# Plain float32 output projections and query products in a two-layer diffusion block, with the low parts of the blocks done ahead on VectorE

## The chip, the cores and the metric

The kernel runs on one core of one Trainium2 chip. The metric is the device time of one execution in microseconds; the numbers shown are medians of several executions, and one execution was also taken by the hardware profiler. The core has five engines with a queue of instructions each: TensorE (PE; its weight loads appear as PEld), VectorE (DVE), ScalarE (ACT), GpSimd (POOL) and SyncE (SP). An engine takes its queue in order; engines wait for one another through semaphores, and data is moved by 16 DMA engines.

## The reference

A backbone with two layers over 512 latent tokens and 256 context tokens of 1024 numbers, all in float32. Layer 0 mixes tokens by a state-space model (S5), layer 1 by latent attention with 8 heads (MLA). Behind each mixer stands an output projection, a residual layer norm, and a channel mixer (PEER) that picks 16 of 16384 experts for each of 8 heads. Cut to what matters here:

```python
def s5_output(y, w_glu, w_o):
    y = gelu(y)
    return (y * sigmoid(y @ w_glu)) @ w_o            # output projection of layer 0
o_lat = attend(...).reshape(b, n, 1024) @ w_o         # output projection of layer 1
h = layer_norm(ALPHA * h + mod[2] * o, ln_g, ln_b)

def peer_route(t, w_q, keys):                         # t = h * (1 + mod[4]) + mod[3]
    q = (t @ w_q).reshape(n, 8, 2, 64)                # queries
    s = einsum('thsd,hsnd->thsn', q, keys)
    sv, si = top_k(s, 16)                             # per half, then over the 256 sums
    ...                                               # expert indices e, gates g = softmax
act = gelu(einsum('td,tkd->tk', t, u[e])) * g
out = einsum('tk,tkd->td', act, v[e])
```

Tokens are worked on in six tiles of 128: tiles 0 and 1 are the context (in layer 0 alone), 2 to 5 the latent tokens.

## The kernel before

**Split products.** A product on TensorE can be made from float32 operands as they are (plain), or from operands in a reduced float32 form (`F32R`). For accuracy the kernel splits an operand for the second way into a high part, a cast on ScalarE (L305), and a low part, the operand less the high part (L306), on an engine that the caller names. `split` holds both lines:

```python
        self.nc.scalar.copy(out=hi, in_=x)
        lo_eng.tensor_tensor(out=lo, in0=x, in1=hi.bitcast(F32), op=ALU.subtract)
```

A split product is then three products into one accumulator: high by high, high by low and low by high.

**Experts.** Some token tiles get their experts by gathering rows with indirect DMAs that GpSimd issues (L1275), a row for each token and expert; VectorE multiplies each row (L1282 for `u`, L1287 for `v`). The others are dense: their scores against all 16384 experts are computed in 128 blocks (`dense_u`, L1137, split products), multiplied with a gate matrix that is made from one-hots (`gate_matrix`: VectorE makes `e` at L1080 and `o` at L1088, TensorE multiplies them at L1102), and multiplied with all of `v` (L1207). Layer 0 gathers tiles 0 and 1 and has tiles 2 to 5 dense; layer 1 gathers tile 5 and has 4, 2 and 3 dense.

**Ahead.** The scores of the first 40 (layer 0) or 48 (layer 1) dense blocks are done ahead, while routing and the gate matrices still run (`ahead`, two blocks of preload). For each, U is loaded, its high part cast by ScalarE and its low part made by GpSimd. The later blocks, in the dense stage, have theirs made by VectorE (`dense_u_prep` with `V`).

**Output projection** (`out_steps`), for a pair of tiles: a first step splits the operands of the pair (`ys` in layer 0 with low parts on GpSimd, `os` in layer 1 with low parts on VectorE). Then 16 steps, two column halves by eight blocks of k: load 128x512 of the weights (`wo`, ring of 8 buffers), split it (`Wos`, low part on VectorE for every fourth step, else GpSimd), three products for each tile of the pair (L799). VectorE multiplies each finished half with a row (L806), and a last step does the residual and the layer norm on VectorE and ScalarE.

**Queries** (`query_steps`), for a pair: `modulate` transposes and modulates each tile's `h` (`mT`) and splits it into the block `Hs` that the dense stage uses too (for the context, into a block `Hc` of its own). Then for each of 8 heads: load 128 columns of weights (`wq`, ring `row` of 5 buffers, which the gathered rows use too), split them with GpSimd's low part, and 24 products of 256 columns, both tiles of the pair side by side (L945).

**Order.** `pipeline(steps, LT)` runs the loads and splits of a step three steps before its products. The list of steps is written out by hand: in layer 0 the projections `o0` (context), `o1` (tiles 2, 3) and `o2` (tiles 4, 5), the gates `g2` to `g5` of the mixer, modulations `m` and heads `q`, with constants E0, E1, E2, YB and YC saying where one list is cut to let another in. `merge` interleaves this stream with the routing of the tiles (`route`, almost all on VectorE: the top-16 searches L972 to L976 and one-hots L1041 to L1047), and, on the side, the blocks ahead and the gate matrices, by estimated times that steps return. The compiler's scheduler then orders each engine's queue; routing, norms, splits and one-hots share VectorE's.

Of the kernel before, what the change touches and what calls it, by code (L numbers as in the profile page):

```python
# [21 lines left out]
KD = 8  # L22
# [33 lines left out]
E0, E1, E2 = 0, 11, 5  # L56
YB, YC = 1, 17
# [50 lines left out]
class Net:  # L108
# [662 lines left out]
    def out_steps(self, l, pair, src, parts, first, rows):  # L771

# [3 lines left out]

        def begin(_):
            st["y"] = parts()
            return 0.0

        def prep(hf, k):
            if (hf, k) == (1, 0):
                st["h"] = []
                for ti in pair:
                    h = self.t4([128, D], "h")
                    self.load(h, first(ti))
                    st["h"].append(h)
            w = self.t2([128, 512], "wo")
            self.load(w, src[k * 128:(k + 1) * 128, hf * 512:(hf + 1) * 512])
            W = self.t4([128, 2, 512], "Wos", F32R)  # L790
            self.split(W[:, 0], W[:, 1], w, nc.gpsimd if k % 4 else nc.vector)
            return W

        def work(hf, k, W):
            if k == 0:
                st["op"] = [self.ps([128, 512], "op") for _ in pair]
            for i, op in enumerate(st["op"]):
                for n, (x, y) in enumerate(((0, 0), (0, 1), (1, 0))):
                    nc.tensor.matmul(out=op, lhsT=st["y"][k // 2][:, x, k % 2, i * 128:(i + 1) * 128], rhs=W[:, y],  # L799
                                     start=(k == 0 and n == 0), stop=(k == KD - 1 and n == 2))  # L800
            if k == KD - 1:
                if hf == 0:
                    st["t"] = [self.t4([128, D], "res") for _ in pair]
                c = slice(hf * 512, (hf + 1) * 512)
                for t, op in zip(st["t"], st["op"]):
                    nc.vector.tensor_tensor(out=t[:, c], in0=op, in1=rows()[0][:, c], op=ALU.mult)  # L806
            return 1.3

        def norm(_):
            for ti, h, t in zip(pair, st["h"], st.pop("t")):  # L810
# [7 lines left out]
        return ([(lambda: None, begin)]  # L818
                + [(lambda hf=hf, k=k: prep(hf, k), lambda W, hf=hf, k=k: work(hf, k, W)) for hf in range(2) for k in range(KD)]
                + [(lambda: None, norm)])  # L820

    def s5_layer(self, dense, gather):
# [25 lines left out]
        def out(pair):  # L848
            s = 1 if pair[0] < 2 else 0
            per = (2, 4)[s]  # L850
            r0 = pair[0] * 128 - (256, 0)[s]

            def parts():
                ys = []
                for x in range(4):
                    ys.append(self.t4([128, 2, 2, 256], "ys", F32R))
                    y = self.yT[s][2 * x // per][:, 2 * x % per:2 * x % per + 2, r0:r0 + 256]
                    self.split(ys[-1][:, 0], ys[-1][:, 1], y, nc.gpsimd)
                return ys

            return self.out_steps(0, pair, a["s5_w_o"], parts,
# [16 lines left out]
        Hc = self.t16([128, 2, KD, 256], "Hc", F32R)  # L878
        self.h1 = {}
        (m0, q0), (m1, q1), (m2, q2) = (self.query_steps(0, (0, 1), lambda: Hc),  # L880
# [5 lines left out]
        steps += g4 + g5[:2 - YB] + o1[:1] + g5[2 - YB:]  # L886
        steps += [(lambda: None, memory)] + o1[1:YC] + o2[:1] + o1[max(YC, 1):] + o2[1:E1] + m1 + o2[E1:] + q1[:E2] + m2 + q1[E2:] + q2
# [20 lines left out]
    def query_steps(self, l, pair, H):  # L908
# [7 lines left out]
        def modulate(i, ti):  # L916
            mT = self.mod_transpose(self.h1[pair][i], l, s, 3)
            c = slice(i * 128, (i + 1) * 128)
            H_ = H()
            self.split(H_[:, 0, :, c], H_[:, 1, :, c], mT, nc.vector)  # L920
            if ti not in self.tiles:
# [8 lines left out]
        def prep(h):  # L930
            w = self.row([128, KD, 128], "wq")
            self.load(w, self.a["peer_w_q"][l, h])
            W = [self.t4([128, KD, 128], f"wq{x}", F32R) for x in range(2)]
            self.split(W[0], W[1], w, nc.gpsimd)
            return W

        def work(h, W):
# [4 lines left out]
            n = 0  # L942
            for k in range(KD):
                for x, y in ((0, 0), (0, 1), (1, 0)):
                    PE.matmul(out=st["p"][:, h % 2], lhsT=W[x][:, k, :], rhs=H()[:, y, k, :], start=(n == 0),  # L945
                              stop=(n == 3 * KD - 1))
                    n += 1
# [195 lines left out]
    def ahead(self, l, n, n_tiles):  # L1143
# [12 lines left out]
        yield from pipeline([(lambda b=b: self.dense_u_prep(l, b, self.nc.gpsimd), lambda Us, b=b: work(b, Us))  # L1156
# [180 lines left out]
    def mla(self, dense, gather):  # L1337
# [181 lines left out]
        def out(pair):  # L1519
            q0 = (min(pair) - 2) * 128  # L1520

            def parts():
                os = []
                for o in oT:
                    os.append(self.t4([128, 2, 2, 256], "os", F32R))
                    for i, ti in enumerate(pair):
                        c = slice(i * 128, i * 128 + 128)
                        self.split(os[-1][:, 0, :, c], os[-1][:, 1, :, c], o[:, :, (ti - 2) * 128:(ti - 1) * 128], V)
                return os

            return self.out_steps(1, pair, a["mla_w_o"], parts, lambda ti: self.hd[ti], lambda: r)
# [91 lines left out]
```

## Time and profile before

| what | value |
|---|---|
| median of 3 executions | 4076.9 us (4074.23 to 4081.48) |
| the profiled execution's own time | 4075.69 us |
| its span | 4073.6 us |
| busy share of the span: PE, PEld, DVE, ACT, POOL | 90%, 74%, 79%, 38%, 40% |
| mean granted TensorE clock (share of full speed) | 0.953 |
| DMA | 986.15 MB, 242 GB/s over the span |

The span falls into stages: the state-space mixer of layer 0 until about 374 us; gates, projections and queries of layer 0 with the first routings until 657; routing of the dense tiles with blocks ahead until 855; gate matrices and blocks ahead until 1110; the dense stage until about 2350; the attention of layer 1 until 2672; its projections and queries until 2765; routing until 2975; gate matrices until 3165; the dense stage until the end.

How to read the views. The table of stretches gives the busy time of each engine in a stretch, the granted TensorE clock and the mean busy share of the 16 DMA engines. A group of instructions has a line, engine, operation, names and shape, a count, its busy time and the mean of one, and the idle time of the engine just before its members with what ended most of it. The timeline has start, length, engine, line, operation, names and shape, with like neighbours merged (x is their count) and the idle time before them in brackets. A plain float32 product shows as two records of TensorE.

### The profile page before, as it was taken

To read this page: it belongs to the slowest core of one execution; us is meant where nothing else is said; L and a number is where in the kernel's file an instruction comes from. 1 tells how busy PE (TensorE), PEld (TensorE's weight loads), DVE (VectorE), ACT (ScalarE), POOL (GpSimd) and SP (SyncE) were. 2 spreads that over 40 slices of the span, in tenths; PEclk is the share of its full clock that TensorE was granted. 3 is DMA by queue.
4 is the path that set the end of the run, shared out by engine and by line. 5 is a ranking of instruction groups with operands and counts; after the bars stand their busy time and mean duration, and the time that the engine had idled before them with its cause. 6 is when DMAs were issued, how large, how long until landed. Compare 5 with 4: busy or idle time off the path is not lost.

```text
span 4073.6 us, 54069 instructions
## 1 busy us (share of the span) xinstructions
PE 3664.2 (90%) x18795; PEld 3029.0 (74%) x18795; DVE 3231.9 (79%) x6315; ACT 1558.1 (38%) x2804; POOL 1638.1 (40%) x1140
## 2 busy tenths in 40 slices
PE   5759879789789999999999989989888899999998
PEld 3527868678667888778888855568888678999997
DVE  8784498988877788988888844469987678888887
ACT  1321335357632322233332233354467333433333
POOL 4744346245412455556555300055344113334341
PEclk6879989899999999999999999999899999999999
DMA  5457234268988899999999820044377888887885
GB/s 178 136 175 249 86 122 156 90 220 272 326 302 293 300 341 342 332 352 340 338 336 342 324 103 3 30 160 149 126 232 256 316 277 321 295 336 283 335 294 215
DMA packets 398450, 986.15 MB, mean 242 GB/s; under 512 B 67040, under 2 KB 147424, under 8 KB 393568
## 3 DMA queue, kind: packets, MB, share of 16 engines
q1 hardware_dynamic: 217120, 501.34, 35.3%
q0 software_dynamic: 110592, 402.70, 28.0%
q10 hardware_dynamic: 70464, 78.65, 5.6%
q8 instruction: 148, 2.42, 0.2%
q14 instruction: 126, 1.03, 0.1%
HBM read 892.28 MB, written 90.21 MB: 241 GB/s over the span
## 4 chain that ended last, share of the span: by engine, by line
PE 45%; issue 10%; DVE 10%; DMA 5%; POOL 5%; ACT 3%; ACTq 0%; POOLq 0%; DVEq 0%; SPq 0%
PE s_ps L1137 20%; PE acc L1207 15%; POOL row L1275 4%; PE g_ps L1102 3%; DMA row<-in_peer_v,idx 2%; DMA W<-in_peer_v 1%; DVE row L1282 1%; PE op_mla L1507 1%; DMA ge<-ged 1%; DVE e L1080 1%; DVE Ws L306 1%; PE acc L1228 1%; DVE f L1287 1%; PE kvp L1365 1%; ACT o L1085 1%
## 5 line engine op out<-in xcount | busy, mean ns | idle before, releaser
L1207 PE MATMUL acc<-Ws,A 128*128 128x512 f32 x5208 | 1202.9, 392 | 63.6 <-ACT A L305 36.3
L1137 PE MATMUL s_ps<-Hs,Uh 128*128 128x512 f32 (+1 forms) x4096 | 1184.8, 371 | 11.2 <-ACT Uh L305 11.2
L1207 PEld LDWEIGHTS acc<-Ws,A 128*128 128x128 f32 x5208 | 981.8, 189 | 280.4 <-ACT A L305 37.0
L1137 PEld LDWEIGHTS s_ps<-Hs,Uh 128*128 128x128 f32 x4096 | 761.5, 190 | 104.9 <-ACT Uh L305 12.6
L1275 POOL DMA_INDIRECT row<-in_peer_u,idx x384 | 513.2, 1336 | 783.2 <-DVE row L1282 712.3
L1137 PE MATMUL s_ps<-Hs,Ul 128*128 128x512 f32 (+1 forms) x2048 | 756.9, 370 | 15.5 <-POOL Ul L306 15.5
L1275 POOL DMA_INDIRECT row<-in_peer_v,idx x384 | 485.6, 1264 | 549.0 <-DVE f L1287 484.8
L1282 DVE SCALAR_TENSOR_TENSOR row<-row,m 128x1024 f32<-128x1024 f32 x384 | 490.4, 1293 | 54.7 <-DMA row<-in_peer_u,idx 53.8
L1287 DVE SCALAR_TENSOR_TENSOR f<-row,act,f 128x1024 f32<-128x1024 f32 x381 | 487.3, 1279 | 39.4 <-DMA row<-in_peer_v,idx 38.4
L305 ACT CAST Ws<-W 128x512 fp32r<-128x512 f32 x512 | 305.5, 619 | 489.0 <-DMA W<-in_peer_v 439.5
L1137 PEld LDWEIGHTS s_ps<-Hs,Ul 128*128 128x128 f32 x2048 | 389.0, 190 | 66.2 <-POOL Ul L306 19.8
L306 DVE TENSOR_TENSOR Ws<-W,Ws 128x512 fp32r<-128x512 f32 x512 | 345.1, 684 | 101.6 <-ACT Ws L305 101.0
L305 ACT CAST Uh<-U 128x1024 fp32r<-128x1024 f32 x256 | 268.1, 1048 | 313.6 <-DMA U<-in_peer_uT 242.6
L306 POOL TENSOR_TENSOR Ul<-U,Uh 128x1024 fp32r<-128x1024 f32 x88 | 227.3, 2585 | 312.3 <-ACT Uh L305 199.0
L1140 ACT ACTIVATE ge<-s_ps 128x512 f32<-128x512 f32 (+1 forms) x256 | 139.1, 544 | 520.4 <-PE s_ps L1137 504.9
L1102 PE MATMUL g_ps<-o,o 128*128 128x128 f32 x1792 | 232.7, 289 | 87.2 <-DVE o L1088 51.7
L1102 PEld LDWEIGHTS g_ps<-o,o 128*128 128x128 f32 x1792 | 223.7, 202 | 96.9 <-ACT o L1085 95.1
L306 POOL TENSOR_TENSOR Wos<-wo,Wos 128x512 fp32r<-128x512 f32 x60 | 87.0, 1476 | 469.9 <-PE tp_ps L286 350.9
L305 ACT CAST A<-ge 128x512 fp32r<-128x512 f32 (+1 forms) x256 | 144.5, 565 | 280.7 <-DVE ge L1188 266.6
L306 DVE TENSOR_TENSOR Ul<-U,Uh 128x1024 fp32r<-128x1024 f32 x168 | 204.9, 1221 | 47.9 <-ACT Uh L305 47.5
L1188 DVE TENSOR_TENSOR ge<-ge,Gt 128x512 f32<-128x512 f32 (+1 forms) x256 | 155.7, 619 | 74.8 <-ACT ge L1140 51.1
L306 DVE TENSOR_TENSOR A<-ge,A 128x512 fp32r<-128x512 f32 (+1 forms) x256 | 158.4, 620 | 45.6 <-ACT A L305 44.7
(346 smaller groups left out, 4631.7 us busy)
## 6 DMA issues: line engine op xcount, KB each, us to landing
U<-in_peer_uT SPq DMA_DIRECT2D x256, 512.0 KB
W<-in_peer_v SPq DMA_DIRECT2D x512, 256.0 KB
gm<-stage ACTq DMA_DIRECT2D x28, 2048.0 KB
ada_wt<-in_ada_w SPq DMA_DIRECT2D x96, 512.0 KB
Gt<-gm SPq DMA_DIRECT2D x16, 2048.0 KB
Gt<-gm SPq DMA_DIRECT2D x16, 1536.0 KB
wq<-in_peer_w_q SPq DMA_DIRECT2D x40, 512.0 KB
wo<-in_s_w_o SPq DMA_DIRECT2D x48, 256.0 KB
```

The source lines that it names most:

```text
L305: self.nc.scalar.copy(out=hi, in_=x)
L306: lo_eng.tensor_tensor(out=lo, in0=x, in1=hi.bitcast(F32), op=ALU.subtract)
L1080: V.tensor_tensor(out=e.rearrange("p s t (i x) -> p (s t) i x", x=2), in0=self.iota128.rearrange("p (i x) -> p i x", x=2).unsqueeze(1).to_ ...
L1085: S.copy(out=o2, in_=e[:, 0])
L1102: PE.matmul(out=gp[:, t, :], lhsT=o[1][:, t4 * 4 + t, :], rhs=o[0][:, t4 * 4 + t, :], start=True, stop=True)
L1137: PE.matmul(out=sp, lhsT=x[:, k, :], rhs=self.Hs[:, y, k, :], start=(n == 0), stop=(n == 3 * KD - 1))
L1140: S.activation(out=ge, in_=sp, func=AF.Gelu)
L1188: V.tensor_tensor(out=gv, in0=gv, in1=Gt[b // SB][:, :, :, b % SB, :], op=ALU.mult)
L1207: PE.matmul(out=acc[hf][d], lhsT=A[b][:, x, c], rhs=Ws[:, y], start=(j == 0 and n == 0), stop=(j == SB - 1 and n == 2))
L1275: GP.indirect_dma_start(out=r, out_offset=None, in_=tab, in_offset=bass.IndirectOffsetOnAxis(ap=ik[:, k:k + 1], axis=0), element_offset=l ...
L1282: x = V.scalar_tensor_tensor(out=r, in0=r, scalar=1.0, in1=m, op0=ALU.mult, op1=ALU.mult, accum_out=act[:, k:k + 1])
L1287: x = V.scalar_tensor_tensor(out=f, in0=r, scalar=act[:, k:k + 1], in1=f, op0=ALU.mult, op1=ALU.add)
```

## The change

It does three things. The output projections multiply plain float32 operands: no operand or weight is split, and one product stands for three. The queries too: 16 products of 128 columns for a head, one tile of the pair after the other, from `mT` and the loaded weights. `mT` is still split into `Hs` for the dense tiles; the context is not split any more, and its block `Hc` goes. The low parts of the U blocks done ahead are made on VectorE. The order constants follow the step list, which has no step for the operands any more.

```diff
-E0, E1, E2 = 0, 11, 5
-YB, YC = 1, 17
+E0, E1, E2 = 0, 10, 5
@@ out_steps
-        def begin(_):
-            st["y"] = parts()
-            return 0.0
...
             self.load(w, src[k * 128:(k + 1) * 128, hf * 512:(hf + 1) * 512])
-            W = self.t4([128, 2, 512], "Wos", F32R)
-            self.split(W[:, 0], W[:, 1], w, nc.gpsimd if k % 4 else nc.vector)
-            return W
+            return w
...
             for i, op in enumerate(st["op"]):
-                for n, (x, y) in enumerate(((0, 0), (0, 1), (1, 0))):
-                    nc.tensor.matmul(out=op, lhsT=st["y"][k // 2][:, x, k % 2, i * 128:(i + 1) * 128], rhs=W[:, y],
-                                     start=(k == 0 and n == 0), stop=(k == KD - 1 and n == 2))
+                nc.tensor.matmul(out=op, lhsT=y(i, k), rhs=W, start=(k == 0), stop=(k == KD - 1))
@@ s5_layer
-        Hc = self.t16([128, 2, KD, 256], "Hc", F32R)
...
-        steps += g4 + g5[:2 - YB] + o1[:1] + g5[2 - YB:]
-        steps += [(lambda: None, memory)] + o1[1:YC] + o2[:1] + o1[max(YC, 1):] + o2[1:E1] + m1 + o2[E1:] + q1[:E2] + m2 + q1[E2:] + q2
+        steps += g4 + g5 + [(lambda: None, memory)] + o1[:16] + o2[:1] + o1[16:] + o2[1:E1] + m1 + o2[E1:]
+        steps += q1[:E2] + m2 + q1[E2:] + q2
@@ query_steps, modulate
-            mT = self.mod_transpose(self.h1[pair][i], l, s, 3)
-            c = slice(i * 128, (i + 1) * 128)
-            H_ = H()
-            self.split(H_[:, 0, :, c], H_[:, 1, :, c], mT, nc.vector)
-            if ti not in self.tiles:
+            mT = st[i] = self.mod_transpose(self.h1[pair][i], l, s, 3)
+            if ti in self.tiles:
+                c = slice(i * 128, (i + 1) * 128)
+                H_ = H()
+                self.split(H_[:, 0, :, c], H_[:, 1, :, c], mT, nc.vector)
+            else:
@@ query_steps, prep and work
-            W = [self.t4([128, KD, 128], f"wq{x}", F32R) for x in range(2)]
-            self.split(W[0], W[1], w, nc.gpsimd)
-            return W
+            return w
...
-            n = 0
-            for k in range(KD):
-                for x, y in ((0, 0), (0, 1), (1, 0)):
-                    PE.matmul(out=st["p"][:, h % 2], lhsT=W[x][:, k, :], rhs=H()[:, y, k, :], start=(n == 0),
-                              stop=(n == 3 * KD - 1))
-                    n += 1
+            for i in range(2):
+                for k in range(KD):
+                    PE.matmul(out=st["p"][:, h % 2, i * 128:(i + 1) * 128], lhsT=W[:, k, :], rhs=st[i][:, k, :],
+                              start=(k == 0), stop=(k == KD - 1))
@@ ahead
-        yield from pipeline([(lambda b=b: self.dense_u_prep(l, b, self.nc.gpsimd), lambda Us, b=b: work(b, Us))
+        yield from pipeline([(lambda b=b: self.dense_u_prep(l, b, self.nc.vector), lambda Us, b=b: work(b, Us))
```

In both layers the helper `out` passes the unsplit tile (`y_tile` in layer 0, `oT` in layer 1) as `y(i, k)` where it passed the function that split it.

## Rows read from the trace of the kernel before

**Rows 1.** Stretches: us, PE, PEld, DVE, ACT, POOL busy (count), clock, DMA share, GB/s.

```profile
489.00:657.00 168.00, 131.81 (x872) 116.41 (x873) 148.25 (x530) 69.72 (x125) 74.09 (x42) 0.91 0.33 109
657.00:855.00 198.00, 170.04 (x925) 142.05 (x923) 193.67 (x910) 77.91 (x116) 81.24 (x37) 0.93 0.36 116
855.00:1110.00 255.00, 216.52 (x1358) 192.93 (x1359) 217.24 (x231) 182.11 (x338) 132.63 (x76) 0.96 0.88 295
...
2672.00:2729.00 57.00, 50.45 (x220) 39.48 (x218) 36.35 (x52) 36.76 (x69) 35.69 (x23) 0.97 0.45 153
...
2765.00:2975.00 210.00, 181.27 (x1108) 173.03 (x1107) 198.57 (x917) 95.18 (x149) 90.68 (x40) 0.91 0.44 140
```

**Rows 2.** Durations of `e` and `o` on VectorE, whole span: min/median/max ns.

```profile
L1080 DVE TENSOR_TENSOR e<-iota,iT x112: 1200/1218/3421, 746.7 to 3141.8; 128x2048 bf16<-128x2048 bf16 x112
...
L1088 DVE TENSOR_TENSOR o<-e,gT x112: 932/958/3136, 748.0 to 3143.1; 128x768 f32<-128x768 bf16 x112
```

**Rows 3.** Groups on VectorE, 855 to 1110: count, busy us, mean ns, idle before.

```profile
L1282 DVE SCALAR_TENSOR_TENSOR row<-row,m 128x1024 f32<-128x1024 f32 x58 | 87.7, 1524 | 9.5 <-DMA row<-in_peer_u,idx 9.5
L1080 DVE TENSOR_TENSOR e<-iota,iT 128x2048 bf16<-128x2048 bf16 x57 | 76.1, 1335 | 17.2 <-ACT iT L1070 17.2
L1088 DVE TENSOR_TENSOR o<-e,gT 128x768 f32<-128x768 bf16 x58 | 61.7, 1064 | 9.8 <-PE s_ps L1137 3.9
```

**Rows 4.** Groups on VectorE, 1400 to 1800.

```profile
L1282 DVE SCALAR_TENSOR_TENSOR row<-row,m 128x1024 f32<-128x1024 f32 x36 | 43.0, 1217 | 5.6 <-DMA row<-in_peer_u,idx 5.6
```

**Rows 5.** Chain that ended last: start, us, what; rates of split and plain products.

```profile
1868.59 43.53 PE acc L1207 x192
...
2491.26 5.42 PE op_mla L1507 x12
```

**Rows 6.** Timeline of TensorE, 433 to 680: gating product, o1's first and last, queries.

```profile
433.31 7.31 PE L762 MATMUL zp<-yl,wg 128*128 128x128 f32 x64
...
535.63 0.51 PE L799 MATMUL op<-Wos,ys 128*128 128x512 f32 x1
...
570.70 5.96 PE L799 MATMUL op<-Wos,ys 128*128 128x512 f32 x25 [1.35 <-DVE Wos L306]
...
665.80 14.51 PE L945 MATMUL qp<-Hs,wq 128*128 128x256 f32 x120
```

**Rows 7.** Timeline of VectorE, 527 to 592: one-hot adds, o1's row product.

```profile
527.47 1.56 DVE L1046 TENSOR_TENSOR oh<-oh 128x512 bf16<-128x512 bf16 x4
...
578.39 8.76 DVE L1046 TENSOR_TENSOR oh<-oh 128x1024 bf16<-128x1024 bf16 x6
...
590.56 1.27 DVE L806 TENSOR_TENSOR res<-op,m 128x512 f32<-128x512 f32 x2
```

**Rows 8.** The page's groups of the U blocks' splits, whole span.

```profile
L305 ACT CAST Uh<-U 128x1024 fp32r<-128x1024 f32 x256 | 268.1, 1048 | 313.6 <-DMA U<-in_peer_uT 242.6
L306 POOL TENSOR_TENSOR Ul<-U,Uh 128x1024 fp32r<-128x1024 f32 x88 | 227.3, 2585 | 312.3 <-ACT Uh L305 199.0
...
L306 DVE TENSOR_TENSOR Ul<-U,Uh 128x1024 fp32r<-128x1024 f32 x168 | 204.9, 1221 | 47.9 <-ACT Uh L305 47.5
```

**Rows 9.** Stretches, instructions on `Ul` alone: PE, PEld, DVE, POOL busy (count).

```profile
657.00:855.00 198.00, 70.64 (x176) 33.66 (x176) 0.00 (x0) 58.39 (x23) 0.93 0.36 116
855.00:1110.00 255.00, 55.17 (x140) 26.35 (x140) 0.00 (x0) 43.42 (x17) 0.96 0.88 295
...
2765.00:2975.00 210.00, 79.61 (x221) 44.44 (x222) 0.00 (x0) 70.75 (x28) 0.91 0.44 140
2975.00:3165.00 190.00, 55.80 (x163) 31.31 (x163) 0.00 (x0) 54.76 (x20) 0.95 0.78 258
```

**Rows 10.** Groups on VectorE, 657 to 855: the compare of routing.

```profile
L1041 DVE TENSOR_TENSOR oh<-iota,ab 128x2048 bf16<-128x2048 bf16 x8 | 13.9, 1764 | 0.0
```

**Rows 11.** Groups on VectorE, 2765 to 2975: the compare of routing.

```profile
L1041 DVE TENSOR_TENSOR oh<-iota,ab 128x2048 bf16<-128x2048 bf16 x8 | 16.1, 2035 | 0.0
```

**Rows 12.** Groups on VectorE, 2975 to 3165: the compare of the gate matrices.

```profile
L1080 DVE TENSOR_TENSOR e<-iota,iT 128x2048 bf16<-128x2048 bf16 x37 | 58.4, 1580 | 26.1 <-ACT iT L1070 25.0 <-PE s_ps L1137 1.2
```

More of the change, by code (lines that the diff above doesn't have):

```diff
@@ L769, in glu, with out_steps @@
             nc.vector.tensor_tensor(out=y, in0=y, in1=sg[:, x * per:(x + 1) * per, :], op=ALU.mult)
-    def out_steps(self, l, pair, src, parts, first, rows):
+    def out_steps(self, l, pair, src, y, first, rows):
         nc = self.nc
         st = {}
-        def begin(_):
-            st["y"] = parts()
-            return 0.0
         def prep(hf, k):
@@ L816, in norm @@
             return 0.0
-        return ([(lambda: None, begin)]
-                + [(lambda hf=hf, k=k: prep(hf, k), lambda W, hf=hf, k=k: work(hf, k, W)) for hf in range(2) for k in range(KD)]
+        return ([(lambda hf=hf, k=k: prep(hf, k), lambda W, hf=hf, k=k: work(hf, k, W)) for hf in range(2) for k in range(KD)]
                 + [(lambda: None, norm)])
@@ L848, in out @@
         def out(pair):
[L849 to L861, printed above, removed]
+            return self.out_steps(0, pair, a["s5_w_o"], lambda i, k: self.y_tile(pair[i], k),
                                   lambda ti: a["ctx"][0, ti * 128:(ti + 1) * 128, :] if ti < 2
@@ L876, in memory_ctx @@
             return 0.0
-        Hc = self.t16([128, 2, KD, 256], "Hc", F32R)
         self.h1 = {}
-        (m0, q0), (m1, q1), (m2, q2) = (self.query_steps(0, (0, 1), lambda: Hc),
+        (m0, q0), (m1, q1), (m2, q2) = (self.query_steps(0, (0, 1), None),
                                         self.query_steps(0, (2, 3), lambda: self.Hall[:, :, :, 0:256]),
@@ L1519, in out @@
         def out(pair):
[L1520 to L1531, printed above, removed]
+            return self.out_steps(1, pair, a["mla_w_o"],
+                                  lambda i, k: oT[k // 2][:, k % 2, (pair[i] - 2) * 128:(pair[i] - 1) * 128],
+                                  lambda ti: self.hd[ti], lambda: r)
         p, q = tuple(order[:2]), tuple(order[2:])
```

## The prediction

> **What bounds the kernel now.** I read the page's engine table and slices first, then the table of stretches, then the tensor engine's order of work around the changed products, then VectorE's in the same stretches, and last the groups of instructions by duration. The change touches two windows, one in each layer: from about 408 to 1110 us and from 2672 to 3165 us. The dense expert stages behind them are bound by TensorE and, early on, by transfers; none of their instructions change, so I move them as a block with whatever comes before.
>
> In the stretches VectorE is what is full: 193.7 of 198 us between 657 and 855, 198.6 of 210 between 2765 and 2975 [rows 1]. That is the routing (top-16 searches). TensorE has room there: 170 of 198 and 181 of 210. In the gate stretch behind (855 to 1110) VectorE and TensorE have 217 of 255 each, and the transfers are at 0.88 [rows 1]. No engine alone bounds it; I read its counterpart in layer 1, 2975 to 3165, in the same way.
>
> The second thing to see is that VectorE's durations in these stretches are not its own. The one-hot compare `e` takes 1218 ns as a median and up to 3421 [rows 2]; in 855 to 1110 its mean is 1335, `o` has 1064 against a median of 958, and a gathered row's product 1524 [rows 3], against 1217 between 1400 and 1800 [rows 4], where GpSimd issues row fetches alone. In the stretches in question it also makes low parts of splits.
>
> **Term 1: products on TensorE.** 192 split products of 512 columns took 43.53 us, 226.7 ns each; a plain float32 product of 512 columns shows as two records, and 12 records took 5.42 us, 903 ns a product [rows 5]. Per step (one tile, one k, one half) the change puts one for three: 903 for 680, +223 ns. There are 16 steps for each of ten tiles: +35.7 us of TensorE time, 21.4 in layer 0 and 14.3 in layer 1. A query head took 24 products of 256 columns: 120 in 14.51 us, so 2.90 us. It becomes 16 products of 128 columns, the shape of the gating product `zp`: 64 records (32 products) in 7.31 us, so 3.65 us [rows 6]. That is +0.75 on 40 heads, +30 us. In all TensorE gets 66 us more work.
>
> **Term 2: what goes.** 80 weight splits, 28 operand splits, 40 query weight splits and two context splits leave ScalarE, GpSimd and VectorE. What counts is where TensorE waited for them. In o1 (tiles 2, 3) the 96 products, 21.8 us by rate, spread from 535.6 until 576.7 [rows 6], because every fourth weight split stood on VectorE behind routing. Then its output row product stood behind routing too and began at 590.56, although the products had ended 14 us before [rows 7]. Behind it come the norm, the transposes, the queries, and the next routing.
>
> I walk this anew. Context first: o0 is 28.9 instead of 21.8 us, q0 29.2 instead of 23.2, and the split of the context operand (some 2 us ahead of q0) goes: routing of the context tiles starts about 6 later, at 495. o1 then runs some 541 to 570 without waiting for splits. VectorE reaches the output product of o1 at 590.6 + 6, less five weight splits (4.5 us), less what GpSimd stretched: six adds of one-hots took 8.76 us, where four of the six had taken 1.56 [rows 7]; with the compares ahead of them, some 10 us. So 582; norm and transposes until 596; the rest of o2 (6 x 1.8) until 607; five heads of q1 until 625; transposes of the second pair; three heads until 640; routing of tile 2 from about 644 instead of 657. **-13 us.** Bounds: 0, if VectorE's order keeps the norm late, and -25, if the norm goes ahead of routing as soon as o1 ends.
>
> **Term 3: the low parts of the U blocks.** 88 of them go from GpSimd (2585 ns) to VectorE, where 168 others take 1221 ns [rows 8]. VectorE gets 23 in 657 to 855, 17 in 855 to 1110, 28 in 2765 to 2975 and 20 in 2975 to 3165 [rows 9]: 28, 21, 34 and 24 us. Against this stands the stretching, which goes with GpSimd's last split. In 855 to 1110: 58 x 307 + 57 x 117 + 58 x 106 ns = 30.6 us [rows 2 to 4]. The same subtraction over the groups of the other stretches (eight groups in each routing stretch, first the compare of that shape with 8 x 546 and 8 x 817 ns; three in the last, first 37 x 362 ns) gives 26, 24 and 32 us [rows 10 to 12]. The net on VectorE is +2, -10, +10 and -8 us.
>
> The Trainium skill, "SBUF — State Buffer", section "Who interferes with whom", says that a VectorE instruction with two SBUF inputs and a GpSimd instruction that reads SBUF exclude each other, and that the later one fully blocks for the earlier one's whole length. The longest `e` is 2.2 us over its median, close to one of GpSimd's splits. By that rule all of the stretching goes; if the rule were not the cause, none of it would, which is the third rival below.
>
> In the routing stretches VectorE is the bound and I count the net in full: **+2** and **+10**. In the gate stretches it is one of three nearly full resources and I count some 7 of 10 and 5 of 8: **-7** and **-5**; bounds 0 and the full -10 and -8. The order constants only follow the step list, which is one shorter: in o2's place ahead of o1's norm stands its first weight step (1.8 us) instead of its operand splits. The row fetches that GpSimd issues in the gate stretches get a free queue, but they wait for VectorE to free row buffers, so I count nothing for it (and 0 to -5 as bounds).
>
> **Term 4: layer 1's start.** Output projection of both pairs is 57.8 us of plain products where it took 57 with its stalls [rows 1]. The query weights no longer wait for a split, and the norm of the first pair hides under ten steps of the second. The first pair's queries end some 4 us later than before: **+4**, bounds 0 and +12. The second pair's end comes 10 later, but its routing waits for VectorE anyway.
>
> **Term 5: new waits.** On VectorE a low part now waits for ScalarE's cast of the high part, with routing, one-hots and row products queued behind it, and TensorE, ScalarE and the row buffers behind these. In the dense stage the same pair of instructions cost VectorE 47.5 us over 168, 0.28 each [rows 8]. Over the 51 of the routing stretches that is 14; I take **+3**, since there the queue of casts is seldom the latest, with bounds 0 and 54 (one whole cast of 1048 ns each time [rows 8]). The weight tiles `wo` and `wq` now stay until their product, in rings of 8 and 5 buffers with three steps of preload; SP's queue waits for these buffers, with the next weights behind. A step takes 1.8 us, a head 3.65, which leaves the three preloads 5 and 11 us; I count nothing, up to +5.
>
> **Sum.** -13 + 2 - 7 + 4 + 10 - 5 + 3 = -6 us. The profiled execution took 4075.7 us with a span of 4073.6; the median of three was 4076.9. From the profiled one: 4069.7, so **4070 us**. What the measurement can tell from no change is 0.2%, 8 us; the forecast lies just inside it.
>
> **Rivals.**
> 1. *VectorE waits for the casts* (slower). The low parts are in VectorE's queue of routing; each that comes before its cast holds all that follows. For: it is full there, so nothing absorbs the wait, and ScalarE itself waits for VectorE's one-hots and for TensorE. Against: 0.28 us in the dense stage. At 0.5 us on each of 51 it is +26, less the 3 counted: 4093. It decides from about 0.2 us each, where it eats the gain.
> 2. *The chain gains in full.* The norm goes ahead of routing (-25 instead of -13), the gate stretches give -18 instead of -12, no new waits: 4070 - 12 - 6 - 3 - 4 (layer 1 without delay) = 4045; with TensorE's clock, granted at 0.91 in 489 to 657 and 2765 to 2975 [rows 1], kept up by steadier work, 4035.
> 3. *The stretching is not GpSimd's.* Then VectorE gains nothing for its 107 us, and the routing stretches alone become 28 and 34 longer where +12 was counted: +50, and no -12 in the gates; with o1's 10 gone, near 4140. Against: in the stretches where GpSimd only issues row fetches the same row product takes 1217 [rows 4].
> 4. *TensorE's 66 us are on the path.* If the projections and queries set the pace with no stall saved, 4075.7 plus layer 0's 39 less 8 and layer 1's 27 less 8: near 4125. Against: 36 us idle on TensorE in 489 to 657 alone [rows 1].
>
> **How the numbers follow.** Forecast 0.45 (its own range 4056 to 4084; of it 0.20 faster by over 0.2%, 0.20 within, 0.05 slower). Rival 1: 0.22 (0.02 within). Rival 2: 0.22, all faster. Rivals 3 and 4: 0.03 and 0.08, slower. Faster 0.42, within 0.22, slower 0.36. The range leaves out the far ends of rivals 1 and 2 and all of 3 and 4: 4038 to 4100.
>
> **What would show it.** Plain products at 903 and 114 ns a record; o1 without gaps and its row product before 585; the routing of tile 2 before 650; `e`, `o` and the row products at their medians in 855 to 1110, with no GpSimd compute. Wrong, if VectorE shows idle before low parts of over 0.3 us each (rival 1), if the first dense stage starts over 25 us earlier or at all later, or if layer 1's first routing starts over 10 us later.

## The result, and the profile after

| | before | after |
|---|---|---|
| median of 5 executions, us | 4076.9 (4074.23 to 4090.13) | 4102.9 (4098.01 to 4115.63) |
| ratio, 95% interval | | 1.0063, 1.0039 to 1.0086 |
| span of the profiled execution, us | 4073.6 | 4101.0 |
| granted TensorE clock over the span | 0.953 | 0.957 |

The change makes the kernel 0.63% slower, 26 us. The forecast was 4070 us, the range 4038 to 4100: both are missed, on the slow side.

I cut the span at events that both traces have: the first score product of tile 2 (layer 0) or of the first routed tile (layer 1), the last step of routing, and the last product of the gate matrices. The differences of the stretches add up to that of the spans, +27.4 us:

| stretch | before, us | after, us | difference | forecast |
|---|---|---|---|---|
| until routing of tile 2 begins | 654.9 | 633.1 | -21.8 | -13 |
| routing, layer 0 | 189.5 | 190.0 | +0.5 | +2 |
| gate matrices, layer 0 | 251.7 | 284.6 | **+32.9** | -7 |
| to the first product with `v` | 38.7 | 41.1 | +2.4 | 0 |
| dense stage, layer 0 | 1219.0 | 1212.9 | -6.1 | 0 |
| attention of layer 1 | 318.3 | 319.4 | +1.1 | 0 |
| projections and queries, layer 1 | 90.3 | 88.3 | -2.0 | +4 |
| routing, layer 1 | 208.2 | 214.7 | +6.5 | +10 |
| gate matrices, layer 1 | 182.0 | 193.0 | **+11.0** | -5 |
| rest | 921.0 | 923.9 | +2.9 | 0 |

(The forecast's +3 for new waits lay on the two routing stretches together.) Everything up to the end of routing in layer 0 came out as well as forecast or better; the two gate stretches lose 43.9 us where 12 were to be won. The stretches of after that answer to [rows 1], same columns:

```profile
489.00:641.00 152.00, 146.85 (x956) 113.40 (x955) 117.52 (x565) 38.56 (x76) 0.00 (x0) 0.98 0.40 131
641.00:833.00 192.00, 169.34 (x916) 140.77 (x915) 182.91 (x886) 71.86 (x107) 5.78 (x6) 0.94 0.39 123
833.00:1120.00 287.00, 226.03 (x1374) 200.03 (x1374) 211.55 (x254) 185.88 (x340) 89.18 (x60) 0.93 0.78 258
2681.00:2739.00 58.00, 57.98 (x154) 26.80 (x153) 17.59 (x33) 10.54 (x23) 0.00 (x0) 1.00 0.43 145
2771.00:2984.00 213.00, 183.37 (x1163) 175.06 (x1162) 200.76 (x939) 88.84 (x140) 4.70 (x5) 0.94 0.41 133
2984.00:3190.00 206.00, 170.93 (x1132) 168.33 (x1132) 144.06 (x164) 133.33 (x242) 43.26 (x32) 0.94 0.75 249
```

In 833 to 1120 no engine is fuller than before: VectorE is busy for 211.6 of 287 us where it had 217.2 of 255. The stretch is longer because they stand. Where VectorE stands is in its groups there (columns as in [rows 3]):

```profile
L1255 DVE SCALAR_TENSOR_TENSOR row<-row,m 128x1024 f32<-128x1024 f32 x60 | 72.4, 1218 | 4.3 <-DMA row<-in_peer_u,idx 4.3
L1053 DVE TENSOR_TENSOR e<-iota,iT 128x2048 bf16<-128x2048 bf16 x59 | 71.9, 1219 | 0.6 <-ACT iT L1043 0.6
L1061 DVE TENSOR_TENSOR o<-e,gT 128x768 f32<-128x768 bf16 x59 | 56.5, 958 | 6.3 <-DVE e L1053 0.5
L305 DVE TENSOR_TENSOR Ul<-U,Uh 128x1024 fp32r<-128x1024 f32 x17 | 20.8, 1226 | 64.3 <-ACT Uh L304 64.3
```

Two things are to be seen. The means of `row`, `e` and `o`, 1524, 1335 and 1064 ns in [rows 3], are at their medians: the stretching has gone with GpSimd's splits, as term 3 had it. And 17 low parts have 64.3 us of idle time in front, all for ScalarE's cast of the same block. The waits in four stretches (engine and line, what it waited for: total us, times, longest) say that this happens in the gate stretches. First 833 to 1120:

```profile
PEld g_ps L1075 <- ACT o L1058: 68.4, 36, 7.4
DVE Ul L305 <- ACT Uh L304: 64.3, 17, 9.0
PE g_ps L1075 <- ACT o L1058: 43.8, 31, 6.3
ACT o L1058 <- DVE e L1053: 37.5, 23, 4.0
...
ACT stage L1077 <- PE g_ps L1075: 23.3, 57, 1.6
```

Then the low parts' line in 641 to 833, in 2771 to 2984 and in 2984 to 3190:

```profile
DVE Ul L305 <- ACT Uh L304: 3.1, 2, 1.7
...
DVE Ul L305 <- ACT Uh L304: 7.1, 5, 3.1
...
DVE Ul L305 <- ACT Uh L304: 53.7, 20, 4.3
```

10 us of waits in the routing stretches, 118 in the gate stretches. The first of the two fences also names a ring: VectorE waits for ScalarE's cast, ScalarE's `stage` copies wait for TensorE's gate products, those wait for ScalarE's conversion of `o`, and this waits for VectorE's `e`. Two of these waits were shorter before, in 855 to 1110 (L1085 and L1102 are after's L1058 and L1075):

```profile
PE g_ps L1102 <- ACT o L1085: 24.8, 24, 2.2
...
ACT o L1085 <- DVE e L1080: 13.4, 14, 2.9
```

One turn of the ring in the timeline, VectorE first, then ScalarE:

```profile
944.55 0.96 DVE L1061 TENSOR_TENSOR o<-e,gT 128x768 f32<-128x768 bf16 x1
954.55 1.23 DVE L305 TENSOR_TENSOR Ul<-U,Uh 128x1024 fp32r<-128x1024 f32 x1 [9.04 <-ACT Uh L304]
955.69 1.22 DVE L1255 SCALAR_TENSOR_TENSOR row<-row,m 128x1024 f32<-128x1024 f32 x1
956.83 0.08 DVE L1255 DVE_READ_ACCUMULATOR row<-row,m 128x1 f32 x1
956.83 1.22 DVE L1053 TENSOR_TENSOR e<-iota,iT 128x2048 bf16<-128x2048 bf16 x1
```

```profile
945.96 1.05 ACT L1058 CAST o<-e 128x1024 f32<-128x1024 bf16 x1
946.90 0.69 ACT L1064 ACTIVATE o<-e,gT 128x128 f32<-128x128 bf16 x2
947.50 0.57 ACT L1077 COPY stage<-g_ps 128x512 f32<-128x512 f32 x1
948.42 0.59 ACT L1077 COPY stage<-g_ps 128x512 f32<-128x512 f32 x1 [0.35 <-PE g_ps L1075]
949.31 0.59 ACT L1077 COPY stage<-g_ps 128x512 f32<-128x512 f32 x1 [0.31 <-PE g_ps L1075]
949.79 1.05 ACT L1058 CAST o<-e 128x1024 f32<-128x1024 bf16 x1
950.74 0.69 ACT L1064 ACTIVATE o<-e,gT 128x128 f32<-128x128 bf16 x2
952.09 0.59 ACT L1077 COPY stage<-g_ps 128x512 f32<-128x512 f32 x1 [0.66 <-PE g_ps L1075]
952.98 0.59 ACT L1077 COPY stage<-g_ps 128x512 f32<-128x512 f32 x1 [0.31 <-PE g_ps L1075]
953.46 1.05 ACT L304 CAST Uh<-U 128x1024 fp32r<-128x1024 f32 x1
...
958.09 1.05 ACT L1058 CAST o<-e 128x1024 f32<-128x1024 bf16 x1 [3.57 <-DVE e L1053]
```

VectorE has finished an `o` at 945.5 and comes to `Ul`, whose cast stands behind the eleven other instructions of ScalarE shown ahead of it. That queue runs in order, for 1.6 us of the time waiting for TensorE, and for 9 us VectorE makes no `e`: the next one starts at 956.83. ScalarE, done with the cast, then stands for 3.57 us until it can convert that `e`, and TensorE's gate products wait for the conversion. So the loss does not stay on VectorE.

**Theory 1**: in the gate stretches each low part stands on VectorE behind a cast that is held in ScalarE's queue; the wait, not VectorE's added work, is the loss. Rivals, numbered as in the expectations below: TensorE's longer products (theory 2); the added work itself (theory 3).

### The profile page after: what moved, and what is told of

It is laid out like the page before. It is cut to its first block, busy times and chain, and to the rows that moved or that the text cites. A ratio compares the mean times of both kernels' runs of the same rounds, so it can differ in the third digit from the quotient of the medians.

```text
span 4101.0 us, 53725 instructions
## 1 busy us (share of the span) xinstructions
PE 3714.2 (91%) x18955; PEld 3028.3 (74%) x18955; DVE 3140.5 (77%) x6364; ACT 1468.5 (36%) x2653; POOL 1205.7 (29%) x940
## 4 chain that ended last, share of the span: by engine, by line
PE 54%; issue 15%; DVE 14%; POOL 7%; DMA 6%; ACT 2%; SPq 1%; POOLq 0%; ACTq 0%; DVEq 0%
PE s_ps L1110 19%; PE acc L1180 14%; POOL row L1248 6%; PE qp L919 4%; PE op L790 3%; DMA row<-in_peer_v,idx 2%; PE g_ps L1075 2%; PE zp L761 2%; DMA W<-in_peer_v 1%; DVE Ul L305 1%; PE op_mla L1480 1%; DMA ge<-ged 1%; DVE w L644 1%; PE yp L696 1%; DVE Ws L305 1%
## 5 line engine op out<-in xcount | busy, mean ns | idle before, releaser
L1248 POOL DMA_INDIRECT row<-in_peer_u,idx x384 | 512.5, 1335 | 2139.8 <-DVE row L1255 1271.8
L1255 DVE SCALAR_TENSOR_TENSOR row<-row,m 128x1024 f32<-128x1024 f32 x384 | 461.3, 1218 | 38.8 <-DMA row<-in_peer_u,idx 38.0
L305 DVE TENSOR_TENSOR Ul<-U,Uh 128x1024 fp32r<-128x1024 f32 x256 | 312.0, 1220 | 175.0 <-ACT Uh L304 172.5
L304 ACT CAST Uh<-U 128x1024 fp32r<-128x1024 f32 x256 | 267.7, 1048 | 299.8 <-DMA U<-in_peer_uT 231.7
L1075 PE MATMUL g_ps<-o,o 128*128 128x128 f32 x1792 | 241.3, 294 | 114.3 <-ACT o L1058 72.0
L1075 PEld LDWEIGHTS g_ps<-o,o 128*128 128x128 f32 x1792 | 230.7, 207 | 126.1 <-ACT o L1058 124.5
L1058 ACT CAST o<-e 128x1024 f32<-128x1024 bf16 x112 | 117.3, 1048 | 88.6 <-DVE e L1053 85.5
L1077 ACT COPY stage<-g_ps 128x512 f32<-128x512 f32 x224 | 125.6, 584 | 62.3 <-PE g_ps L1075 60.8
```

The costliest lines, as they stand in the source:

```text
L1075: PE.matmul(out=gp[:, t, :], lhsT=o[1][:, t4 * 4 + t, :], rhs=o[0][:, t4 * 4 + t, :], start=True, stop=True)
L1077: S.copy(out=stage[:, :, c:c + 4], in_=gp.rearrange("p t i -> p i t"))
L1248: GP.indirect_dma_start(out=r, out_offset=None, in_=tab, in_offset=bass.IndirectOffsetOnAxis(ap=ik[:, k:k + 1], axis=0), element_offset=l ...
L1255: x = V.scalar_tensor_tensor(out=r, in0=r, scalar=1.0, in1=m, op0=ALU.mult, op1=ALU.mult, accum_out=act[:, k:k + 1])
```

## The experiments

All ratios are against runs of the kernel before on the same chip. Stretches are those above, of each kernel's profiled execution (us; "R0" until routing of tile 2 begins):

| kernel | median, us | ratio (95%) | R0 | routing 0 | gates 0 | routing 1 | gates 1 |
|---|---|---|---|---|---|---|---|
| before | 4076.9 | 1 | 654.9 | 189.5 | 251.7 | 208.2 | 182.0 |
| after | 4102.9 | 1.0063 (1.0039 to 1.0086) | 633.1 | 190.0 | 284.6 | 214.7 | 193.0 |
| e1_pool_low | 4058.2 | 0.9947 (0.9932 to 0.9963) | 634.1 | 187.4 | 252.7 | 210.8 | 182.4 |
| e2_low_only | 4135.3 | 1.0145 (1.0128 to 1.0163) | 654.0 | 195.2 | 283.9 | 215.6 | 195.2 |
| e3_hybrid | 4053.2 | 0.9947 (0.9934 to 0.9960) | 632.8 | 190.1 | 253.7 | 211.5 | 183.4 |
| e4_cast_dve | 4074.6 | 0.9993 (0.9984 to 1.0002) | 631.5 | 202.1 | 254.8 | 223.6 | 181.5 |
| e5_la4 | 4112.3 | 1.0088 (1.0074 to 1.0103) | 629.5 | 200.0 | 279.7 | 220.1 | 189.0 |
| e6_out_only | 4056.9 | 0.9957 (0.9944 to 0.9970) | 637.3 | 190.0 | 252.4 | 209.0 | 181.3 |
| e7_query_only | 4065.7 | 0.9972 (0.9961 to 0.9983) | 650.1 | 188.6 | 251.6 | 210.8 | 184.1 |
| e8_cast_gate | 4061.3 | 0.9950 (0.9936 to 0.9963) | 633.2 | 190.0 | 257.2 | 215.6 | 182.8 |
| e9_out_hybrid | 4067.7 | 0.9967 (0.9955 to 0.9979) | 634.7 | 194.0 | 253.4 | 214.1 | 181.6 |
| e10_low_lag | 4043.9 | 0.9904 (0.9889 to 0.9920) | 633.8 | 195.6 | 247.9 | 209.4 | 171.8 |
| e11_before_lag | 4073.6 | 0.9982 (0.9972 to 0.9992) | 653.6 | 198.8 | 247.8 | 208.9 | 172.8 |

(The kernel before had medians of 4076 to 4081 beside them; where a few us matter, kernels that ran at different times are compared by ratio. The profiled execution of e5 took 4101.2 us, 11 less than its median, that of e4 4082.1, 7.5 more.)

**e1_pool_low: the change without its third part.**

```diff
-self.dense_u_prep(l, b, self.nc.vector)
+self.dense_u_prep(l, b, self.nc.gpsimd)
```

> The changed kernel with the low parts of the blocks done ahead on GpSimd again; projections and queries stay plain. Theory 1 (in the gate stretches VectorE stands ahead of low parts until ScalarE has cast the high part, and ScalarE stands behind TensorE and VectorE; 118 us of such waits): the start of layer 0's routing stays some 20 us earlier than in the kernel before, the gate stretch of layer 0 is back at about 250 us (285 in the changed kernel), layer 1's at about 182 (193): 4060 us, 4045 to 4070. Theory 2 (the plain products' 66 us of TensorE time are what is paid): 4090 or more. Theory 3 (the low parts' own 107 us on VectorE are what is paid, not a wait): as theory 1 here.

4058.2: the plain products alone are 0.53% faster than before, and the gate stretches are as long as before. With GpSimd's splits the stretching is back as well (822 to 1074 of this kernel):

```profile
L1255 DVE SCALAR_TENSOR_TENSOR row<-row,m 128x1024 f32<-128x1024 f32 x56 | 87.3, 1569 | 5.8 <-DMA row<-in_peer_u,idx 5.8
L1053 DVE TENSOR_TENSOR e<-iota,iT 128x2048 bf16<-128x2048 bf16 x60 | 75.5, 1258 | 16.7 <-ACT iT L1043 16.3 <-PE g_ps L1075 0.4
L1061 DVE TENSOR_TENSOR o<-e,gT 128x768 f32<-128x768 bf16 x60 | 63.5, 1058 | 12.9 <-PE s_ps L1110 4.5 <-POOL Ul L305 2.3 <-ACT o L1064 0.5
```

So TensorE's longer products cannot be the loss: they are all in here. Theory 2 is out.

**e2_low_only: the third part alone.**

```diff
-self.dense_u_prep(l, b, self.nc.gpsimd)
+self.dense_u_prep(l, b, self.nc.vector)
```

> The kernel before with one part of the change alone: the low parts of the blocks done ahead on VectorE; projections and queries stay split. Theory 1: both gate stretches get longer by about what they got in the changed kernel (33 and 11 us), and the gain at the start of routing is missing: 4115 us, 4105 to 4135, with over 100 us of VectorE idle ahead of low parts. Theory 2: no slower than the kernel before, 4065 to 4080. Theory 3: 4115 too, but without more idle time ahead of low parts than 0.3 us each.

4135.3, at the top of theory 1's range. The gate stretches take 283.9 and 195.2 us, with 66.3 and 51.5 us of waits before low parts, far over the 0.3 us each of theory 3: the loss belongs to the low parts, whatever the products. Some 13 us more are lost in the two routing stretches, which are 5.7 and 7.4 us longer than before.

**e4_cast_dve: the wait taken away, work added.** VectorE makes the high parts of the blocks ahead too.

```diff
-        self.split(Uh, Ul, U, lo_eng)
+        if lo_eng is self.nc.vector and b < self.n_ahead:
+            lo_eng.tensor_copy(out=Uh, in_=U)
+            lo_eng.tensor_tensor(out=Ul, in0=U, in1=Uh.bitcast(F32), op=ALU.subtract)
+        else:
+            self.split(Uh, Ul, U, lo_eng)
```

> The changed kernel with the high part of the blocks ahead made on VectorE as well, just ahead of the low part, so that VectorE waits for no cast of ScalarE; VectorE gets 88 casts more (some 0.6 to 1.2 us each). Theory 1: the idle time ahead of low parts is gone, the gate stretch of layer 0 falls from 285 to 265 us or less although VectorE has some 17 us more work there; the routing stretches get longer by the casts, 20 to 30 us each; in all about 4100, 4080 to 4120. Theory 3: the gate stretch gets longer still, 295 to 305 us, and the whole is 4140 or more.

VectorE works more, and the gate stretches are 254.8 and 181.5 again; the low parts ahead, in the trace's groups on VectorE, wait for almost nothing:

```profile
L1100 DVE TENSOR_TENSOR Ul<-U,Uh 128x1024 fp32r<-128x1024 f32 x88 | 107.3, 1220 | 3.7
```

Theory 3 falls for the gate stretches. In routing, where VectorE is full, its casts cost 12 and 9 us, where 20 to 30 each were expected; that takes back half of the 41 us that the gate stretches give back. The time, 4074.6, is below the expected 4080 to 4120.

**e8_cast_gate: the same, only for the blocks of the gate stretches.**

```diff
-        self.split(Uh, Ul, U, lo_eng)
+        if (23, 28)[l] <= b < self.n_ahead:
+            lo_eng.tensor_copy(out=Uh, in_=U)
+            lo_eng.tensor_tensor(out=Ul, in0=U, in1=Uh.bitcast(F32), op=ALU.subtract)
+        else:
+            self.split(Uh, Ul, U, lo_eng)
```

> The changed kernel; for the blocks ahead that fall into the gate stretches (from the 24th in layer 0, from the 29th in layer 1) VectorE makes the high part too, by a cast of its own, so that no low part waits for ScalarE there; in the routing stretches ScalarE casts as in the change. Theory 1 (the loss is the wait of VectorE for ScalarE in the gate stretches, not the work): the gate stretch of layer 0 goes back from 285 to about 254 us, of layer 1 from 193 to about 182, and the routing stretches keep their 190 and 215: 4102.9 - 31 - 11 = 4061, between 4053 and 4070. Rival (VectorE's work in the gate stretches counts as well, and the cast adds 37 x 1.2 us to it): 4075 to 4100.

4061.3 against 4061 expected from theory 1; the gate stretches take 257.2 and 182.8 (254 and 182 expected).

**e3_hybrid: VectorE for the blocks of the routing stretches, GpSimd for those of the gates.**

```diff
-self.dense_u_prep(l, b, self.nc.vector)
+self.dense_u_prep(l, b, self.nc.vector if b < (23, 28)[l] else self.nc.gpsimd)
```

> The changed kernel, with the low parts on VectorE for the first 23 (layer 0) and 28 (layer 1) blocks ahead, those of the routing stretches, and on GpSimd for the 17 and 20 of the gate stretches. Theory 1: routing as in the changed kernel (end at 823 us), the gate stretch of layer 0 at about 250 us, layer 1's at about 182; VectorE's idle time ahead of low parts of blocks ahead under 15 us: 4062 us, 4050 to 4075. Theory 2: 4090 or more. Theory 3: half of the loss comes back, 4075 to 4090.

4053.2, inside theory 1's range. Both ways of taking the wait away come out alike, 0.9947 here and 0.9950 in e8. It is also what e1 has, with all low parts on GpSimd (0.9947): the move has no gain to show for the blocks of the routing stretches.

**e5_la4: more preload.** `LA` from 2 to 4 blocks.

```diff
-LA, LD = 2, 5
+LA, LD = 4, 5
```

> The changed kernel with four blocks of preload instead of two for the blocks ahead (LA 2 to 4), so that the cast of a block's high part is issued up to two blocks earlier than its products need. Theory 1 in its plain form (the wait is for a cast that comes too late in ScalarE's queue): the 118 us of VectorE idle ahead of low parts in the gate stretches fall to 60 or less, the gate stretch of layer 0 from 285 to 270 or less: 4075 to 4090. Theory 1b (cast and low part move earlier together, so that VectorE stands at the low part as before, whatever the preload): no change, 4095 to 4110, with the same idle time.

4112.3, just above the range of theory 1b and far from that of the plain form. The gate stretches stay long (279.7 and 189.0): that the cast comes late for want of preload is out. The waits of VectorE in 830 to 1110 of this kernel:

```profile
DVE Ul L305 <- ACT Uh L304: 61.1, 16, 9.1
```

In 2985 to 3175 they are 46.0 us. More preload moves cast and low part ahead together, and the wait stays.

**e10_low_lag: the low part issued one block later than its cast.**

```diff
-        yield from pipeline([(lambda b=b: self.dense_u_prep(l, b, self.nc.vector), lambda Us, b=b: work(b, Us))
+        V, low = self.nc.vector, {}
+        def prep(b):
...
+            self.nc.scalar.copy(out=Uh, in_=U)
+            low[b] = lambda: V.tensor_tensor(out=Ul, in0=U, in1=Uh.bitcast(F32), op=ALU.subtract)
+            if b:
+                low.pop(b - 1)()
+            return Uh, Ul
...
+        yield from pipeline([(lambda b=b: prep(b), lambda Us, b=b: product(b, Us))
```

(`product` makes the last low part, if it is still due, before its block's work.)

> The changed kernel, with each low part of a block ahead issued one block later than its cast (the cast of block b, then the low part of block b-1), all on VectorE. Theory 1 says that the low part stands on VectorE because it comes directly behind a cast that is itself held by the one-hots behind it: with a block between the two the waits before low parts in the gate stretches fall from 64 and 54 us to under 30 together, the stretches to about 256 and 185, the time to about 4065 (4055 to 4080). Rival 1c (each engine's order is set by the compiler's own estimates, and the low part ends up as close to its cast as before): waits over 90 us, 4095 to 4110.

4043.9, below the expected range: the fastest of all, 0.96% under before and 1.6% under the change. The waits of the 88 low parts ahead for their casts are down from 128 to 37 us, 17.0 and 20.1 in the two gate stretches (under 30 together were expected), which take 247.9 and 171.8 us (256 and 185 expected). The other groups are at their medians in 829 to 1078:

```profile
L1053 DVE TENSOR_TENSOR e<-iota,iT 128x2048 bf16<-128x2048 bf16 x60 | 73.1, 1219 | 15.4 <-ACT iT L1043 15.4
L1272 DVE SCALAR_TENSOR_TENSOR row<-row,m 128x1024 f32<-128x1024 f32 x56 | 67.6, 1218 | 0.0
...
L1136 DVE TENSOR_TENSOR Ul<-U,Uh 128x1024 fp32r<-128x1024 f32 x17 | 20.8, 1221 | 17.0 <-ACT Uh L1135 17.0
```

The other two waits of the ring are shorter too, in the same stretch:

```profile
PE g_ps L1075 <- ACT o L1058: 22.4, 20, 2.6
...
ACT o L1058 <- DVE e L1053: 9.0, 12, 1.3
```

The work is that of the change (VectorE has 6364 instructions in both); only the distance between cast and low part differs. With the runs above this shows theory 1: the wait is the loss.

**e11_before_lag: the same lag on the kernel before** (split products; the diff is that of e10).

> The kernel before (split projections and queries) with the low parts of the blocks ahead on VectorE, each issued one block later than its cast. The low parts alone, issued directly behind the cast, took 4135 with gate stretches of 284 and 195 us. Theory 1 (in the gate stretches only the wait costs, so that the lag gives back 30 to 36 us in layer 0 and 12 to 23 in layer 1): 4070 to 4095. Rival (the lag gained in the changed kernel only because of how the plain products left ScalarE's queue): 4110 to 4135. Against the run of the changed kernel with the lag (4043.9) the difference is what the plain products give when no wait is left: 30 us if they give what they gave with the wait (4135 to 4103), so 4074.

4073.6 against 4074. The lag gives back 1.6% here too (1.0145 to 0.9982), and the plain products give 0.8% with the wait (1.0145 to 1.0063) as without it (0.9982 to 0.9904). Against before, low parts on VectorE with a lag shorten the gate stretches by 3.9 and 9.2 us and lengthen routing by 9.3 and 0.7: in all 0.18%.

**e6_out_only and e7_query_only: plain projections alone, plain queries alone** (each the hunks of the change that belong to it, on the kernel before).

> The kernel before with the plain output projections alone; queries split, low parts of blocks ahead on GpSimd. Theory A (the gain of the two plain parts, 20 us together, comes from the projections, whose weight splits stood behind routing on VectorE): routing of layer 0's tile 2 starts at 640 or earlier (655 before, 633 with both parts): 4055 to 4062, as good as both parts or better, since a split query head takes 0.75 us less of TensorE. Theory B (both parts are needed, since the query splits keep GpSimd and with it VectorE busy): 4063 to 4072.

> The kernel before with the plain queries alone; projections split, low parts of blocks ahead on GpSimd. Theory A: nothing gained, or slower by up to the queries' 30 us of TensorE time where they are on the path (layer 0's tiles 2 to 5 and layer 1): 4077 to 4095. Theory B: a gain of 5 to 12 us, 4065 to 4072.

The projections alone came out as theory A had it, 0.43% faster; the queries alone as theory B had it, 0.28%. Neither theory holds of both: the projections give most, and the queries give something by themselves. Both together (e1) give 0.53%, less than the sum of 0.71%, but the intervals are too wide to tell the two apart. At the start of tile 2's routing the gains nearly add: 17.6 and 4.8 us alone, 20.8 together.

**e9_out_hybrid: e6 with the low parts of e3.**

> The kernel before with plain output projections alone, queries split as before, and low parts on VectorE for the blocks ahead of the routing stretches only (23 and 28 of them), on GpSimd for the rest. If plain queries give nothing once the projections are plain (4056.9 against 4058.2), this is as fast as the change with the same low parts: 4053, between 4046 and 4060. If plain queries help when GpSimd has no query weights to split beside routing, it is slower than that: 4060 to 4068.

4067.7, 0.9967, where the same with plain queries (e3) had 0.9947. The 4053 is missed, and the time lies in the range of the second case, that plain queries help beside routing. By the ratios the difference is 8 us, with intervals that just overlap; whether split queries disturb the routing stretches (4 and 3 us longer) is left open.

## Why the prediction was wrong

**The step that failed** is in terms 3 and 5 together: term 5 priced the new wait "over the 51 of the routing stretches" and term 3 counted the other 37 low parts as a gain, "some 7 of 10 and 5 of 8". The wait came in the gate stretches, 118 us of it (3.2 each over 37), 10 in routing (0.2 over 51), and turned the -12 of the gate stretches into +43.9. I had looked for where the waiting engine was full. What decides is the queue of the engine that it waits for: ScalarE is busy for 72 of 192 us in routing and for 186 of 287 in the gates, and there it waits itself for TensorE and for VectorE. [rows 1] had it: 77.91 of 198 against 182.11 of 255. Two of the prediction's own signs of being wrong came true: 1.5 us of idle before each low part ahead (128 us over 88), and a dense stage of layer 0 that starts 14 us later.

**The upper bound** of that wait, one cast of 1048 ns [rows 8], was no bound. VectorE waits for all that stands ahead of the cast in ScalarE's queue, 9.04 us in the turn above. The 0.28 us of the dense stages came from a queue that is less full: in that of layer 0, 1110 to 2350 of before, ScalarE is busy for 366 of 1240 us.

**Rival 1** had the mechanism right ("each that comes before its cast holds all that follows") and the place wrong. By its 0.5 us on 51 it gave 4093; the measured time is above that, and outside the range.

**Term 3's contention** was right: 1524, 1335 and 1064 ns went to 1218, 1219 and 958. "SBUF — State Buffer" of the Trainium skill, section "Who interferes with whom", by which a VectorE instruction with two SBUF inputs contends with a GpSimd instruction that reads SBUF, has the trace on its side: with GpSimd's splits back, in e1, the means are 1569, 1258 and 1058 again. But shorter instructions next to a wait give nothing: the change has both. Rival 3 is out. With the wait mostly gone (e10, e11) the gate stretches are 3.8 to 10.2 us shorter than before, about the -7 and -5 of the forecast; in layer 0 routing takes more than that back.

**Term 2** was right in kind and too small, -21.8 for -13 (bounds 0 and -25). The first row product behind o1 starts at 573.53, where I had 582, and before 590.56 [rows 7]; that is 8.5 of the 8.8 us by which the term fell short. TensorE's and VectorE's timelines:

```profile
538.40 24.30 PE L790 MATMUL op<-wo,yl 128*128 128x512 f32 x56
567.86 22.89 PE L790 MATMUL op<-wo,yl 128*128 128x512 f32 x48 [5.15 <-DMA wo<-in_s_w_o]
```

```profile
573.53 0.68 DVE L796 TENSOR_TENSOR res<-op,m 128x512 f32<-128x512 f32 x1
```

o1 runs without gaps to 562.7. Behind it TensorE waits 5.15 us for a weight tile `wo`, about the upper end of what term 5 gave for such waits; it had counted nothing.

**Term 1** had the new rates right. The page's groups of after, busy time over 320 and 1280 records:

```profile
L919 PE MATMUL qp<-mT,wq 128*128 128x128 f32 x1280 | 145.1, 275 | 0.0
L790 PE MATMUL op<-wo,yl 128*128 128x512 f32 x128 | 57.7, 611 | 5.2 <-DMA wo<-in_s_w_o 5.2
L790 PE MATMUL op<-wo,oT 128*128 128x512 f32 x128 | 55.6, 592 | 0.0
L790 PE MATMUL op<-wo,yc 128*128 128x512 f32 x64 | 27.6, 592 | 0.0
```

145.1/40 is 3.63 us a head (3.65 forecast), 57.7/64 is 902 ns a product (903). But the old ones were dearer where they stood than in the dense stage that I took their rate from. The groups of before are 123.3 us for 480 split products of the projections (257 ns each, not 226.7) and 121.0 for the queries:

```profile
L945 PE MATMUL qp<-Hs,wq 128*128 128x256 f32 x768 | 96.0, 285 | 2.3 <-POOL wq L306 2.3
L799 PE MATMUL op<-Wos,ys 128*128 128x512 f32 x288 | 75.6, 420 | 31.2 <-DVE Wos L306 26.0 <-POOL Wos L306 3.1 <-ACT Wos L305 1.1
L799 PE MATMUL op<-Wos,os 128*128 128x512 f32 x192 | 47.7, 404 | 2.5 <-ACT Wos L305 1.3 <-POOL Wos L306 1.2
L945 PE MATMUL qp<-Hc,wq 128*128 128x256 f32 x192 | 25.0, 294 | 1.9 <-ACT Hc L305 1.1 <-DVE Hc L306 0.8
```

So TensorE got 17.6 + 24.1 = 42 us more, not 66. Part of that may be the clock, which was lower there before (last section). Rival 4 falls with e1.

**Term 4**: -2.0 where +4 stood, outside its bounds (0 and +12). The projections of layer 1 took 58.1 us without a stall, 55.6 of them products (57.8 forecast). Before, TensorE waited 5.59 us for VectorE's `h` between query heads, from 2744.9 on; after, it has no wait in that stretch.

**Rival 2**, the chain that gains in full, was priced at 4045, and 4035 with the clock kept up. The change with most of the wait taken away (e10) measures 4043.9, and not far from that rival's terms: it has -21.1 until tile 2's routing (rival: -25), -14.0 in the gate stretches (-18) and +7.3 in routing (+12). So that rival's sum needed a kernel that does not wait, and the change is not it.

## What to carry to other kernels

Before a step is moved to another engine, look at the queue of whoever feeds it: where the producer's queue is busy with work that in turn waits for the new consumer, the pair becomes a ring, and each turn costs what stands ahead of the producer, not what the producer takes: here 3.2 us on average, for a cast of 1.05. Issuing the second half of a two-engine step one iteration later than the first adds no work and broke this ring: 1.6% in two kernels. An engine that gets shorter instructions and longer waits at once can look less busy and be slower, so read the idle column beside the mean.

## What was not expected of the hardware

The granted TensorE clock in the stretch up to tile 2's routing rose from 0.91 (489 to 657 of before, TensorE busy for 131.8 of 168 us) to 0.98 (489 to 641 of after, 146.9 of 152), and in layer 1's projections from 0.97 to 1.00; for the first of these, rival 2 had allowed. In the gate stretch of layer 0, where TensorE waited more, it fell from 0.96 to 0.93 (busy for 216.5 of 255 before and 226.0 of 287 after), and in the kernel with the lag it is back at 0.97. How much of the gains and losses above is the clock's was not measured by itself.
